# A stick-breaking attention block: the causal mask put into the scores' accumulator ahead of the scores, and the order of work planned with measured matmul times

## The chip, the cores and the metric

The kernel runs on one core of a Trainium2 chip. A time is the device time of one execution in microseconds (us). Besides it there is a trace of one profiled execution, and it is this trace that the text reads. The engines are named as the profile names them: PE does the matmuls (PEld is its weight loads), DVE is the vector engine, ACT the scalar engine, POOL is GpSimd, and SP issues most of the loads.

## The reference

One decoder layer on 256 rows of 4096 numbers, all fp32 (only the attention layer is there, since the depth is 1):

```python
def attn_branch(xn, w_in, w_out):
    proj = xn @ w_in                                  # 256x4096 @ 4096x16384
    q, k, v, g = jnp.split(proj, 4, axis=-1)
    o = stick_breaking_attention(heads(q), heads(k), heads(v))   # 32 heads of 128
    return (o * jax.nn.silu(g)) @ w_out               # 256x4096 @ 4096x4096

# stick_breaking_attention, for one block of 128 query rows:
    causal = s_pos[None, :] < t_pos[:, None]
    z = einsum('bhqd,bhkd->bhqk', qb, k) * scale
    log_fail = where(causal, log_sigmoid(-z), 0.0)
    suffix = cumsum(log_fail, reverse=True) - log_fail
    log_a = log_sigmoid(z) + suffix
    a = where(causal, exp(log_a), 0.0)
    o = einsum('bhqk,bhkd->bhqd', a, v)

h = x + attn_branch(rms_norm(x, norm_attn), w_in, w_out)
out = rms_norm(h, final_norm)
```

## The kernel before

**The two large products.** The 16384 columns of w_in are done in 16 units of 1024 columns, the 4096 columns of w_out in 4 units after them. The stationary operands are 128x128 blocks of the normalised rows (or, for w_out, of the gated head outputs), the moving operands are 128x512 blocks of weights. All units but the first of each matrix use Strassen-like forms, with fewer products and some sums of weights and of rows instead. An fp32 operand is split into a high part, rounded to the type that PE multiplies, and a low part, the rest. So a product is three matmuls into one accumulator `acc`: high weights with high rows, low weights with high rows, high weights with low rows. `mm3` issues the three. In the names of the trace, `wh` and `wl` are the high and the low part of the weights, `sh` and `sl` those of the rows in the w_in units, `oh` and `ol` those of the gated heads (`p`) in the w_out units.

**Who makes the operands.** SP loads a block `raw` of weights (a ring of 9 of them), DVE makes sums of blocks (`raw<-raw,raw`), ACT casts `wh<-raw`, and DVE subtracts `wl<-raw,wh`. At the end of a unit DVE and ACT bring the accumulators (`combine`) into `qk_sb` and `gv_sb`, or into `h` in the w_out units. There the residual (`xres`) and the gain (`grow`) are also applied to `h` on DVE, one block after the other.

**The heads.** The two heads of unit u are done while PE works on unit u+1. A head is a chain over PE, ACT and DVE (`head`, and `gated_with` for its gate): four transposes into `tr`, a copy to `qkT` on ACT, the two score matmuls into the accumulator `z`, the causal mask added to two 128x128 blocks of `z` on DVE, softplus and its split into `fh` and `fl`, four matmuls of the suffix sum into the same `z`, the exponential `a`, two transposes of the gate and two matmuls into `o`. So PE's queue gets five insertions of two or four small matmuls for each head, 160 in all. The mask is `never`, a 128x128 tile that holds a very negative number where a key isn't ahead of its query and zero elsewhere.

**What sets the order.** Every engine runs its queue in the order in which the program was written, and that order comes out of a planner (`Plan`): it plays the kernel with a cost for each piece of work (`vector_ns`, `scalar_ns`, `tensor_ns`, and for the small matmuls of the heads `ten`), and on each engine it writes next the waiting work with the lowest key. A key is mostly the place in PE's planned run at which the result is due, less a lead in us: `EARLY` for loads, `CAST_AHEAD` for casts, `SUMS_AHEAD` and `FOURTH_AHEAD` for sums of blocks, `EVICT` for bringing accumulators in, `HEADS_AHEAD` and `HEADS_LATER` for the forms of the heads for w_out. `HEAD_AT` and `GATE_AT` say after which step of unit u+1 the heads and the gate of unit u may begin. `LEAD` is what the planner lets pass between an operand's end and the product that uses it. None of this is in the program that runs: there only the order is left, and the waits on data. Since all work goes through one helper, almost every line of the trace is L167, and instructions are told apart by the tiles they write and read.

Of the kernel before, what the change touches and what calls it, by code (L numbers as in the profile page):

```python
# [14 lines left out]
ALU = mybir.AluOpType  # L15
# [4 lines left out]
P = 128  # L20
S = 256
D = 4096
H = 32
NT = S // P
KC = D // P
CW = 256
HG = CW // P
NB = D // CW
# [18 lines left out]
PAIRS, LOWS = 6, 5  # L47
KEPT = 6
LAST_STEPS = (2,6,5,1,0,7,3,4)
LATE_FROM, LATE_BEHIND = 4,1  # L50
CLOSING = "adebcf"
HEAD_AT = (1,5)
GATE_AT = 1
HEAD_SOON, GATE_SOON = 8.0,8.0

SPREAD = (10, 1.1)
HEADS_AHEAD = 4
HEADS_LATER = 10
AHEAD, SUMS_AHEAD = 1.0,3.0
PIPE = 1  # L60
T3_LEAD = 2000
FOURTH_IN, FOURTH_OUT = (5, 6),()
FOURTH_AHEAD = 10.0
RAW_LEAD = 0
EARLY = 1.5
TEN_WAIT = 1500
LAST_WAIT = 1000
QK_LEAD = 1500
CAST_AHEAD = 3.0
BLOCKS_LATER = 1  # L70
NEVER = -1e30
OUT_ACT = (1, 4, 7)
# [2 lines left out]
FORM_LEAD = 0  # L75
STATS = 2, 6
AWAY, PLACE_H = (0, 1, 2), (0, 1, 0, 1, 0, 2)
EVICT = 1500


PLAIN = {"C11": 1, "C21": 4, "C12": 7, "C22": 6}
# [60 lines left out]


def tensor_ns(n):
    return 0.4167 * n + 13.4 if n > 128 else 109.0


class Plan:
# [7 lines left out]

    TAIL = {"tensor": 190, "vector": 114, "scalar": 125, "gpsimd": 50, "sync": 50}

    LEAD = 195

    class Engine:
        def __init__(self, tc, engine):
# [120 lines left out]
def kernel(  # L283
# [124 lines left out]
        return nc.work("scalar", cost, emit, soon() if key is None else key, **kw)  # L408


    FULL_P, FULL_S = (P,) * 2, (W,) * 2

    def ten(emit, *n, last=False):
        return nc.work(
            "tensor", 90 + sum(tensor_ns(m) for m in n), emit, nc.here - 1e4, wait=LAST_WAIT if last else TEN_WAIT
        )

    def moved(engine, emit, sizes, key, after=None, hold=False, adds=False):
        issue = 700 if engine == "gpsimd" else 330
# [519 lines left out]
    def mm3(out_, a, b, start, stop):  # L939

        (ah, al), (bh, bl) = a, b
        kw = dict(skip_group_check=True)
        nc.tensor.matmul(out_, ah, bh, start=start, stop=False, **kw)
        nc.tensor.matmul(out_, ah, bl, start=False, stop=False, **kw)
        nc.tensor.matmul(out_, al, bh, start=False, stop=stop, **kw)


    BW = 3 * P
    def head(u, i):
        yield nc.take("att", "qkh")  # L950
        tr = att.tile([P, 2, S], F32, tag="att", name=f"tr{u}_{i}")

        def turn():
            for k in range(2):
                for t in range(NT):
                    c = k * CW + i * P
                    nc.tensor.transpose(tr[:, k, t * P : (t + 1) * P], st["qk", u][:, t, c : c + P], ident)

        yield ten(turn, P, P, P, P, last=u == NB - 1)
        if i == HG - 1:  # L960
            nc.give("one")
        qk = ap.tile([P, 2, S], F32, tag="qkh", name=f"qkT{u}_{i}")
        yield act(lambda: nc.scalar.copy(qk, tr), 2 * S)
        nc.give("att")
        yield nc.take("att")
        z = att.tile([P, BW], F32, tag="att", name=f"z{u}_{i}")

        def scores():
            kw = dict(stop=False, skip_group_check=True)
            nc.tensor.matmul(z[:, 0:P], qk[:, 1, P:S], qk[:, 0, P:S], start=True, **kw)  # L970
            nc.tensor.matmul(z[:, P:BW], qk[:, 1, 0:P], qk[:, 0, :], start=False, **kw)

        yield ten(scores, *FULL_P, *FULL_S, last=u == NB - 1)
        nc.give("qkh")
        yield nc.take("f")
        front = z[:, 0 : 2 * P].rearrange("p (a b) -> p a b", a=2)
        both = never.rearrange("p (a b) -> p a b", a=1).broadcast_to([P, 2, P])
        yield dve(lambda: nc.vector.tensor_tensor(out=front, in0=front, in1=both, op=ALU.add), 2 * P)

        f = ap.tile([P, BW], F32, tag="f", name=f"f{u}_{i}")  # L980

        def soft():
            nc.scalar.activation(f, z, AF.Softplus, scale=scale)

        yield act(soft, (BW, TABLE), soon(HEAD_SOON))
        yield nc.take("qkh", "gh", first=True)
        fh = ap.tile([P, BW], F32R, tag="qkh", name=f"fh{u}_{i}")
        fl = wp.tile([P, BW], F32R, tag="gh", name=f"fl{u}_{i}", bufs=3)
        yield act(lambda: nc.scalar.activation(fh, f, AF.Copy, scale=1.0 / scale), BW)
        yield dve(  # L990
            lambda: nc.vector.scalar_tensor_tensor(
                out=fl, in0=f, scalar=1.0 / scale, in1=fh.bitcast(F32), op0=ALU.mult, op1=ALU.subtract
            ),
            BW,
        )
        nc.give("f")

        def scan():
            kw = dict(start=False, skip_group_check=True)
            nc.tensor.matmul(z, neg_tri, fh, stop=False, **kw)  # L1000
            nc.tensor.matmul(z, neg_tri, fl, stop=False, **kw)
            nc.tensor.matmul(z[:, 2 * P : BW], neg_one, fh[:, 0:P], stop=False, **kw)
            nc.tensor.matmul(z[:, 2 * P : BW], neg_one, fl[:, 0:P], stop=True, **kw)

        yield ten(scan, BW, BW, P, P, last=u == NB - 1)
        nc.give("qkh", "gh")
        yield nc.take("f")
        a = ap.tile([P, BW], F32, tag="f", name=f"a{u}_{i}")


        def weights_of():
            nc.scalar.activation(a, z, AF.Relu, scale=-scale)
            nc.scalar.preload_act_table_set("natural_log_exp_and_others")
            nc.scalar.activation(a, a, AF.Exp, scale=-1.0)

        yield act(weights_of, (BW, TABLE, BW))
        nc.give("att")
        nc.start(gated_with(u, i))
        yield nc.until(("gated", u, i))
        o = st["both", u, i][:, 1, :]  # L1020
        v = lambda t: st["gv", u][:, t, i * P : (i + 1) * P]

        def out_of_head():
            kw = dict(skip_group_check=True)
            nc.tensor.matmul(o, v(0), a[:, P:BW], start=True, stop=False, **kw)
            nc.tensor.matmul(o[:, P:S], v(1), a[:, 0:P], start=False, stop=True, **kw)

        yield ten(out_of_head, *FULL_P, *FULL_S, last=u == NB - 1)
        nc.give("f")
        if i == HG - 1:  # L1030
            nc.give("two")
        gated = st["gated", u, i]
        yield dve(lambda: nc.vector.tensor_tensor(out=gated, in0=o, in1=gated, op=ALU.mult), S)
        nc.give("att")

    def gated_with(u, i):
        yield nc.until(("gate", u))
        yield nc.take("att")
        both = st["both", u, i] = att.tile([P, 2, S], F32, tag="att", name=f"o{u}_{i}")
        gT = both[:, 0, :]  # L1040

        def turn():
            for t in range(NT):
                nc.tensor.transpose(gT[:, t * P : (t + 1) * P], st["gv", u][:, t, CW + i * P : CW + (i + 1) * P], ident)

        yield ten(turn, P, P, last=u == NB - 1)
        if i == 0:
            yield nc.take("gh", first=True)
            st["o", u] = wp.tile([P, 4, P], F32, tag="gh", name=f"gated{u}", bufs=3)
        gated = st["gated", u, i] = st["o", u][:, 2 * i : 2 * i + 2, :].rearrange("p a b -> p (a b)")  # L1050
        yield act(lambda: nc.scalar.copy(gated, gT), S)
        nc.tell(("gated", u, i))
# [425 lines left out]
```

## Time and profile before

| what | value |
|---|---|
| time, median of 3 runs | 1715.29 us (1714.85 to 1718.54) |
| span of the profiled execution | 1713.9 us |
| PE busy | 1695.8 us, 99% of the span |
| DVE busy | 1626.6 us, 95% |
| ACT busy | 1299.1 us, 76% |
| POOL busy | 229.2 us, 13% |
| matmuls into acc | 1868 of each of three kinds for w_in, 485 of each of three for w_out |
| DMA | 438.82 MB, mean 256 GB/s |

The profiled execution is a single one: its span runs from the first to the last instruction and is 1.4 us under the median of the timed runs. Busy times overlap, since the engines work beside each other. A matmul's own busy time is longer than the distance to the next one, since PE is a pipeline, so in the timelines the starts of the matmuls are what is to be compared. In a row of a timeline stand the start, the busy time, the engine, the line, the operation with its tiles, and in brackets how long the engine had been idle before it and what ended the wait. A row with "x2" or more is a run of such instructions, with the busy time of all of them.

### The profile page before, as it was taken

To read this page: it belongs to the slowest core of one execution; us is meant where nothing else is said; L and a number is where in the kernel's file an instruction comes from. 1 tells how busy PE (TensorE), PEld (TensorE's weight loads), DVE (VectorE), ACT (ScalarE), POOL (GpSimd) and SP (SyncE) were. 2 spreads that over 40 slices of the span, in tenths; PEclk is the share of its full clock that TensorE was granted. 3 is DMA by queue.
4 is the path that set the end of the run, shared out by engine and by line. 5 is a ranking of instruction groups with operands and counts; after the bars stand their busy time and mean duration, and the time that the engine had idled before them with its cause. 6 is when DMAs were issued, how large, how long until landed. Compare 5 with 4: busy or idle time off the path is not lost.

```text
span 1713.9 us, 24493 instructions
## 1 busy us (share of the span) xinstructions
PE 1695.8 (99%) x7645; PEld 1401.2 (82%) x7645; DVE 1626.6 (95%) x1840; ACT 1299.1 (76%) x1579; POOL 229.2 (13%) x241
## 2 busy tenths in 40 slices
PE   9999999999999999999999999999999999999996
PEld 6888888888888888888888888888888888888885
DVE  7889999999999999999999999999999987899997
ACT  7977878777777787878787778787878875656564
POOL 0001111111111111111101010101111122011000
PEclk9999999999999999999999999999999999999998
DMA  9979898989898989898989897989898888798886
GB/s 303 359 206 261 238 264 242 268 238 272 230 276 234 278 224 284 220 286 220 282 221 287 218 284 221 279 230 267 239 265 247 275 267 247 224 283 261 259 247 236
DMA packets 243764, 438.82 MB, mean 256 GB/s; under 512 B 25616, under 2 KB 47888, under 8 KB 243632
## 3 DMA queue, kind: packets, MB, share of 16 engines
q1 hardware_dynamic: 196752, 354.24, 61.7%
q0 software_dynamic: 45584, 81.15, 26.7%
q10 hardware_dynamic: 1296, 1.85, 0.3%
q8 instruction: 60, 0.98, 0.2%
q14 instruction: 72, 0.59, 0.1%
HBM read 411.45 MB, written 9.96 MB: 246 GB/s over the span
## 4 chain that ended last, share of the span: by engine, by line
PE 96%; DVE 2%; DMA 1%; issue 0%; ACT 0%; SPq 0%; DVEq 0%; ACTq 0%
PE acc L167 91%; PE z L167 2%; PE o L167 2%; PE tr L167 1%; DVE wl L167 1%; DMA raw<-in_w_in_dram 1%; DVE h L167 1%; DMA raw<-in_w_out_dram 0%; SPq L167 0%; ACT sq L167 0%; DVE raw L167 0%; DVE p L167 0%; DVE xs L167 0%; ACT wh L167 0%; DVE back L167 0%
## 5 line engine op out<-in xcount | busy, mean ns | idle before, releaser
L167 ACT CAST wh<-raw 128x1024 fp32r<-128x1024 f32 (+1 forms) x989 | 976.1, 1016 | 323.7 <-PE acc L167 138.6
L167 DVE TENSOR_TENSOR wl<-raw,wh 128x1024 fp32r<-128x1024 f32 (+1 forms) x989 | 1130.6, 1181 | 27.6 <-ACT wh L167 17.4
L167 PE MATMUL acc<-wh,sh 128*128 128x512 f32 x1868 | 745.2, 399 | 0.7 <-ACT wh L167 0.7
L167 PE MATMUL acc<-wh,sl 128*128 128x512 f32 x1868 | 729.5, 391 | 0.4 <-DVE sl L167 0.4
L167 PE MATMUL acc<-wl,sh 128*128 128x512 f32 x1868 | 728.2, 390 | 1.0 <-DVE wl L167 1.0
L167 PEld LDWEIGHTS acc<-wh,sl 128*128 128x128 f32 x1868 | 350.8, 188 | 76.0 <-DVE sl L167 1.0
L167 PEld LDWEIGHTS acc<-wl,sh 128*128 128x128 f32 x1868 | 351.6, 188 | 71.7 <-DVE wl L167 2.5
L167 PEld LDWEIGHTS acc<-wh,sh 128*128 128x128 f32 x1868 | 351.4, 188 | 70.4 <-ACT wh L167 2.2
L167 DVE TENSOR_TENSOR raw<-raw,raw 128x512 f32<-128x512 f32 (+1 forms) x384 | 357.5, 936 | 2.2 <-issue 1.4
L167 POOL DMA_DIRECT2D raw<-in_w_in_dram x120 | 144.2, 1202 | 1073.0 <-DMA raw<-in_w_in_dram 654.6
L167 PE MATMUL acc<-wl,oh 128*128 128x512 f32 x485 | 189.4, 390 | 1.1 <-DVE wl L167 1.0
L167 PE MATMUL acc<-wh,oh 128*128 128x512 f32 x485 | 190.0, 392 | 0.0
L167 PE MATMUL acc<-wh,ol 128*128 128x512 f32 x485 | 189.2, 390 | 0.0
L167 PEld LDWEIGHTS acc<-wl,oh 128*128 128x128 f32 x485 | 91.1, 188 | 21.4 <-DVE wl L167 2.8
L167 PEld LDWEIGHTS acc<-wh,ol 128*128 128x128 f32 x485 | 91.1, 188 | 19.3 <-DVE ol L167 0.5
L167 PEld LDWEIGHTS acc<-wh,oh 128*128 128x128 f32 x485 | 91.1, 188 | 18.7
L167 ACT ACT_TABLE_LOAD x80 | 102.6, 1283 | 1.4
L167 DVE TENSOR_TENSOR gv_sb<-acc,gv_sb 128x512 f32<-128x512 f32 (+1 forms) x60 | 49.3, 822 | 19.5 <-ACT wh L167 18.2
L167 POOL DMA_DIRECT2D raw<-in_w_out_dram x18 | 21.7, 1204 | 162.0 <-DMA raw<-in_w_out_dram 105.4
L167 POOL DMA_DIRECT2D raw<-raw x30 | 26.5, 883 | 83.7 <-DMA raw<-in_w_in_dram 41.3
L167 ACT ACTIVATE qk_sb<-qk_sb,rin_v 128x512 f32<-128x512 f32 x30 | 21.6, 723 | 19.0 <-DVE qk_sb L167 19.0
L167 ACT CAST oh<-p 128x512 fp32r<-128x512 f32 (+3 forms) x41 | 19.5, 488 | 20.0 <-DVE p L167 11.2
(84 smaller groups left out, 666.2 us busy)
## 6 DMA issues: line engine op xcount, KB each, us to landing
raw<-in_w_in_dram SPq DMA_DIRECT2D x1022, 256.0 KB, 5.1
raw<-in_w_out_dram SPq DMA_DIRECT2D x256, 256.0 KB, 5.2
raw<-in_w_in_dram POOLq DMA_DIRECT2D x60, 512.0 KB, 7.9
raw<-in_w_in_dram POOLq DMA_DIRECT2D x60, 256.0 KB, 7.0
raw<-raw POOLq DMA_DIRECT2D x30, 512.0 KB, 7.5
p<-spill POOLq DMA_DIRECT2D x41, 128.0 KB, 4.8
raw<-in_w_out_dram POOLq DMA_DIRECT2D x9, 512.0 KB, 8.9
xr<-in_x_dram SPq DMA_DIRECT2D x16, 256.0 KB, 5.6
```

The lines of the kernel that those rows point to most:

```text
L167: return self.tc.keep_in_program_order(getattr(self.engine, name)(*args, **kw))
```

## The change

Four things change together.

- **The mask.** ACT copies `never` into the two blocks of `z` ahead of the score matmuls, and these accumulate onto it (`start=False`). DVE's addition to `z` is gone. The zone's flags, by which a matmul overwrites or adds, are now left to the transposes of `tr`: their order is another, and the first two of the four carry `start`.
- **The order in `mm3`.** The matmul of the low weights was the second of three and is the last now.
- **The planner's costs.** `tensor_ns` becomes 226.4 ns for 512 columns, the insertions of the heads get a number each (360, 470, 520, 575, 140 ns), and `LEAD` is 0 instead of 195 ns.
- **The planner's leads**, a dozen numbers at the head of the file.

```diff
--- before.py
+++ after.py
@@ -47,26 +47,26 @@
 PAIRS, LOWS = 6, 5
 KEPT = 6
 LAST_STEPS = (2,6,5,1,0,7,3,4)
-LATE_FROM, LATE_BEHIND = 4,1
+LATE_FROM, LATE_BEHIND = 4, 1
 CLOSING = "adebcf"
-HEAD_AT = (1,5)
-GATE_AT = 1
-HEAD_SOON, GATE_SOON = 8.0,8.0
+HEAD_AT = (3, 5)
+GATE_AT = 4
+HEAD_SOON, GATE_SOON = 6.0, 8.0
 
 SPREAD = (10, 1.1)
-HEADS_AHEAD = 4
-HEADS_LATER = 10
-AHEAD, SUMS_AHEAD = 1.0,3.0
+HEADS_AHEAD = 5
+HEADS_LATER = 5
+AHEAD, SUMS_AHEAD = 0.5, 4.0
 PIPE = 1
 T3_LEAD = 2000
 FOURTH_IN, FOURTH_OUT = (5, 6),()
-FOURTH_AHEAD = 10.0
+FOURTH_AHEAD = 14.0
 RAW_LEAD = 0
-EARLY = 1.5
+EARLY = 2.5
 TEN_WAIT = 1500
 LAST_WAIT = 1000
 QK_LEAD = 1500
-CAST_AHEAD = 3.0
+CAST_AHEAD = 5.0
 BLOCKS_LATER = 1
 NEVER = -1e30
 OUT_ACT = (1, 4, 7)
@@ -75,7 +75,7 @@
 FORM_LEAD = 0
 STATS = 2, 6
 AWAY, PLACE_H = (0, 1, 2), (0, 1, 0, 1, 0, 2)
-EVICT = 1500
+EVICT = 500
 
 
 PLAIN = {"C11": 1, "C21": 4, "C12": 7, "C22": 6}
@@ -142,7 +142,7 @@
 
 
 def tensor_ns(n):
-    return 0.4167 * n + 13.4 if n > 128 else 109.0
+    return 226.4 * n / 512
 
 
 class Plan:
@@ -156,7 +156,7 @@
 
     TAIL = {"tensor": 190, "vector": 114, "scalar": 125, "gpsimd": 50, "sync": 50}
 
-    LEAD = 195
+    LEAD = 0
 
     class Engine:
         def __init__(self, tc, engine):
@@ -408,12 +408,8 @@
         return nc.work("scalar", cost, emit, soon() if key is None else key, **kw)
 
 
-    FULL_P, FULL_S = (P,) * 2, (W,) * 2
-
-    def ten(emit, *n, last=False):
-        return nc.work(
-            "tensor", 90 + sum(tensor_ns(m) for m in n), emit, nc.here - 1e4, wait=LAST_WAIT if last else TEN_WAIT
-        )
+    def ten(emit, cost, last=False):
+        return nc.work("tensor", cost, emit, nc.here - 1e4, wait=LAST_WAIT if last else TEN_WAIT)
 
     def moved(engine, emit, sizes, key, after=None, hold=False, adds=False):
         issue = 700 if engine == "gpsimd" else 330
@@ -941,8 +937,8 @@
         (ah, al), (bh, bl) = a, b
         kw = dict(skip_group_check=True)
         nc.tensor.matmul(out_, ah, bh, start=start, stop=False, **kw)
-        nc.tensor.matmul(out_, ah, bl, start=False, stop=False, **kw)
-        nc.tensor.matmul(out_, al, bh, start=False, stop=stop, **kw)
+        nc.tensor.matmul(out_, al, bh, start=False, stop=False, **kw)
+        nc.tensor.matmul(out_, ah, bl, start=False, stop=stop, **kw)
 
 
     BW = 3 * P
@@ -951,12 +947,14 @@
         tr = att.tile([P, 2, S], F32, tag="att", name=f"tr{u}_{i}")
 
         def turn():
-            for k in range(2):
-                for t in range(NT):
-                    c = k * CW + i * P
-                    nc.tensor.transpose(tr[:, k, t * P : (t + 1) * P], st["qk", u][:, t, c : c + P], ident)
-
-        yield ten(turn, P, P, P, P, last=u == NB - 1)
+            for n, (k, t) in enumerate(((1, 0), (0, 0), (0, 1), (1, 1))):
+                c = k * CW + i * P
+                nc.tensor.matmul(
+                    tr[:, k, t * P : (t + 1) * P], st["qk", u][:, t, c : c + P], ident, start=n < 2, stop=True,
+                    is_transpose=True, skip_group_check=True,
+                )
+
+        yield ten(turn, 360, last=u == NB - 1)
         if i == HG - 1:
             nc.give("one")
         qk = ap.tile([P, 2, S], F32, tag="qkh", name=f"qkT{u}_{i}")
@@ -965,17 +963,18 @@
         yield nc.take("att")
         z = att.tile([P, BW], F32, tag="att", name=f"z{u}_{i}")
 
+        front = z[:, 0 : 2 * P].rearrange("p (a b) -> p a b", a=2)
+        both = never.rearrange("p (a b) -> p a b", a=1).broadcast_to([P, 2, P])
+        yield act(lambda: nc.scalar.copy(front, both), 2 * P)
+
         def scores():
-            kw = dict(stop=False, skip_group_check=True)
-            nc.tensor.matmul(z[:, 0:P], qk[:, 1, P:S], qk[:, 0, P:S], start=True, **kw)
-            nc.tensor.matmul(z[:, P:BW], qk[:, 1, 0:P], qk[:, 0, :], start=False, **kw)
-
-        yield ten(scores, *FULL_P, *FULL_S, last=u == NB - 1)
+            kw = dict(start=False, stop=False, skip_group_check=True)
+            nc.tensor.matmul(z[:, 0:P], qk[:, 1, P:S], qk[:, 0, P:S], **kw)
+            nc.tensor.matmul(z[:, P:BW], qk[:, 1, 0:P], qk[:, 0, :], **kw)
+
+        yield ten(scores, 470, last=u == NB - 1)
         nc.give("qkh")
         yield nc.take("f")
-        front = z[:, 0 : 2 * P].rearrange("p (a b) -> p a b", a=2)
-        both = never.rearrange("p (a b) -> p a b", a=1).broadcast_to([P, 2, P])
-        yield dve(lambda: nc.vector.tensor_tensor(out=front, in0=front, in1=both, op=ALU.add), 2 * P)
 
         f = ap.tile([P, BW], F32, tag="f", name=f"f{u}_{i}")
 
@@ -1002,7 +1001,7 @@
             nc.tensor.matmul(z[:, 2 * P : BW], neg_one, fh[:, 0:P], stop=False, **kw)
             nc.tensor.matmul(z[:, 2 * P : BW], neg_one, fl[:, 0:P], stop=True, **kw)
 
-        yield ten(scan, BW, BW, P, P, last=u == NB - 1)
+        yield ten(scan, 520, last=u == NB - 1)
         nc.give("qkh", "gh")
         yield nc.take("f")
         a = ap.tile([P, BW], F32, tag="f", name=f"a{u}_{i}")
@@ -1025,7 +1024,7 @@
             nc.tensor.matmul(o, v(0), a[:, P:BW], start=True, stop=False, **kw)
             nc.tensor.matmul(o[:, P:S], v(1), a[:, 0:P], start=False, stop=True, **kw)
 
-        yield ten(out_of_head, *FULL_P, *FULL_S, last=u == NB - 1)
+        yield ten(out_of_head, 575, last=u == NB - 1)
         nc.give("f")
         if i == HG - 1:
             nc.give("two")
@@ -1043,7 +1042,7 @@
             for t in range(NT):
                 nc.tensor.transpose(gT[:, t * P : (t + 1) * P], st["gv", u][:, t, CW + i * P : CW + (i + 1) * P], ident)
 
-        yield ten(turn, P, P, last=u == NB - 1)
+        yield ten(turn, 140, last=u == NB - 1)
         if i == 0:
             yield nc.take("gh", first=True)
             st["o", u] = wp.tile([P, 4, P], F32, tag="gh", name=f"gated{u}", bufs=3)
```

The queues hold the same instructions as before, but for 32 additions `z<-z,never` that leave DVE and 32 copies `z<-never` of 128x256 that come to ACT. What moves is their order.

On PE, at the ninth block of weights of the first unit (`wh8`, `wl8`; `sh4` and `sl4` are the rows' forms for it), before:

```order
L167 MATMUL acc0_6_197<-wh7_286,sl3_96 128x512
L167 MATMUL acc0_1_130<-wh8_303,sh4_298 128x512
L167 MATMUL acc0_1_130<-wl8_312,sh4_298 128x512
L167 MATMUL acc0_1_130<-wh8_303,sl4_299 128x512
L167 MATMUL acc0_4_170<-wh8_303,sh4_298 128x512
L167 MATMUL acc0_4_170<-wl8_312,sh4_298 128x512
L167 MATMUL acc0_4_170<-wh8_303,sl4_299 128x512
```

and now:

```order
L167 MATMUL acc0_6_197<-wl7_302,sh3_95 128x512
L167 MATMUL acc0_1_130<-wh8_306,sh4_298 128x512
L167 MATMUL acc0_1_130<-wh8_306,sl4_299 128x512
L167 MATMUL acc0_1_130<-wl8_312,sh4_298 128x512
L167 MATMUL acc0_4_169<-wh8_306,sh4_298 128x512
L167 MATMUL acc0_4_169<-wh8_306,sl4_299 128x512
L167 MATMUL acc0_4_169<-wl8_312,sh4_298 128x512
```

In each group of three the matmul of `wl` has gone from the second to the third place, and that of `sl` from the third to the second.

On DVE, at the start of the first unit of w_out (unit 16), while the heads of unit 15 are still to be done, before:

```order
L167 TENSOR_TENSOR gv_sb15_12569<-acc15_3_11942,gv_sb15_12569 128x512
L167 TENSOR_TENSOR wl814_12665<-raw128_10_12553,wh814_12647 128x1024
L167 TENSOR_TENSOR p0_12519<-p0_12519 128x128 x4
L167 TENSOR_TENSOR p1_12527<-p1_12527 128x2x128
L167 TENSOR_TENSOR p2_12626<-p2_12626 128x128 x4
L167 TENSOR_TENSOR z15_0_12732<-z15_0_12732,never_122 128x256
L167 TENSOR_TENSOR ol0_12602<-p0_12519,oh0_12601 128x384
L167 TENSOR_TENSOR ol1_12611<-p1_12527,oh1_12610 128x256
L167 TENSOR_TENSOR ol2_12708<-p2_12626,oh2_12707 128x384
L167 TENSOR_TENSOR wl815_12685<-raw128_11_12562,wh815_12664 128x1024
L167 TENSOR_TENSOR wl816_12697<-raw129_00_12570,wh816_12684 128x1024
```

and now:

```order
L167 TENSOR_TENSOR wl813_12653<-raw128_01_12498,wh813_12631 128x1024
L167 TENSOR_TENSOR gv_sb15_12590<-acc15_5_11937,gv_sb15_12590 128x1024
L167 TENSOR_TENSOR p1_12515<-p1_12515 128x2x128
L167 TENSOR_TENSOR gv_sb15_12590<-acc15_3_11941,gv_sb15_12590 128x512
L167 TENSOR_TENSOR ol0_12601<-p0_12507,oh0_12600 128x384
L167 TENSOR_TENSOR ol1_12612<-p1_12515,oh1_12611 128x256
L167 TENSOR_TENSOR wl814_12670<-raw128_10_12540,wh814_12645 128x1024
L167 TENSOR_TENSOR wl815_12688<-raw128_11_12554,wh815_12669 128x1024
L167 TENSOR_TENSOR ol2_12752<-p2_12684,oh2_12751 128x512
L167 TENSOR_TENSOR wl816_12701<-raw129_00_12570,wh816_12687 128x1024
L167 TENSOR_TENSOR p2_12684<-p2_12684 128x128 x4
L167 TENSOR_TENSOR wl817_12725<-raw129_01_12583,wh817_12698 128x1024
```

`p0` to `p2` are the first blocks of gated heads for w_out. Before, `wl815` stands behind ten additions on `p`, the mask of the first head of unit 15 and three `ol`; now the two additions on `gv_sb15` and two `ol` stand ahead of `wl814`, `wl815` follows it at once, the mask is gone and the additions on `p2` come later.

On DVE, in the second unit of w_out, before:

```order
L167 TENSOR_TENSOR wl863_13833<-raw139_01_13754,wh863_13814 128x1024
L167 TENSOR_TENSOR wl864_13848<-raw138_11_13673,wh864_13831 128x512
L167 TENSOR_TENSOR h0_1_13566<-h0_1_13566,xres0_1_13818 128x512
L167 TENSOR_TENSOR wl865_13867<-raw139_11_13763,wh865_13847 128x1024
L167 TENSOR_TENSOR raw139_00_13712<-raw139_00_13712,raw139_10_13630 128x1024
L167 TENSOR_TENSOR h0_1_13566<-h0_1_13566,grow0_13726 128x512
L167 TENSOR_TENSOR wl866_13878<-raw139_10_13630,wh866_13866 128x1024
L167 TENSOR_TENSOR raw139_11_13763<-raw139_00_13712,raw139_11_13763 128x1024
L167 TENSOR_TENSOR wl867_13910<-raw139_00_13712,wh867_13877 128x1024
```

and now:

```order
L167 TENSOR_TENSOR raw139_00_13712<-raw139_00_13712,raw139_10_13606 128x1024
L167 TENSOR_TENSOR h0_1_13567<-h0_1_13567,xres0_1_13818 128x512
L167 TENSOR_TENSOR wl864_13848<-raw138_11_13673,wh864_13831 128x512
L167 TENSOR_TENSOR wl865_13863<-raw139_11_13766,wh865_13847 128x1024
L167 TENSOR_TENSOR h0_1_13567<-h0_1_13567,grow0_13726 128x512
L167 TENSOR_TENSOR wl866_13875<-raw139_10_13606,wh866_13862 128x1024
L167 TENSOR_TENSOR wl867_13891<-raw139_00_13712,wh867_13874 128x1024
L167 TENSOR_TENSOR raw139_11_13766<-raw139_00_13712,raw139_11_13766 128x1024
L167 TENSOR_TENSOR wl868_13902<-raw140_00_13777,wh868_13888 128x1024
```

The sum `raw139_00` has gone ahead of the addition of `xres0_1`, and the sum `raw139_11` behind `wl867`.

## The prediction

> **What bounds the kernel now.** I read the page first, for the engines and the chain of waits; these are its span, its busy times and the chain:
>
> ```profile
> span 1713.9 us, 24493 instructions
> PE 1695.8 (99%) x7645; PEld 1401.2 (82%) x7645; DVE 1626.6 (95%) x1840; ACT 1299.1 (76%) x1579; POOL 229.2 (13%) x241
> PE 96%; DVE 2%; DMA 1%; issue 0%; ACT 0%; SPq 0%; DVEq 0%; ACTq 0%
> ```
>
> PE holds 96% of the chain that ended last. Then the busy time by stretches (us, then busy time and instructions of PE, PEld, DVE, ACT and POOL, granted clock, DMA share, GB/s):
>
> ```profile
> 0.00:85.00 85.00, 81.61 (x338) 63.00 (x339) 69.07 (x133) 71.46 (x139) 3.68 (x12) 1.00 0.97 331
> 1020.00:1190.00 170.00, 170.00 (x776) 141.24 (x775) 166.11 (x175) 133.57 (x152) 24.20 (x23) 1.00 0.90 249
> 1360.00:1530.00 170.00, 168.93 (x752) 138.48 (x751) 147.26 (x206) 114.15 (x153) 30.24 (x47) 1.00 0.80 247
> 1530.00:1700.00 170.00, 169.97 (x750) 140.36 (x748) 162.59 (x184) 102.03 (x125) 14.40 (x13) 1.00 0.83 250
> ```
>
> In the middle PE has no idle time at all: 170.00 of 170, with the heads' small matmuls in it. So the time is made of PE's own instructions, which the change leaves as they are, and of three other things: the waits of the start (3.4 us of idle in the first 85), some in the w_out units, and 13.9 us behind 1700. DVE, at 166 of 170, has hardly 4 us to spare there, and ACT 36.
>
> **The start.** PE's and DVE's rows show several waits of this kind up to 33 us; the last one is, on PE:
>
> ```profile
> 32.06 0.40 PE L167 MATMUL acc<-wl,sh 128*128 128x512 f32 x1
> 32.83 0.50 PE L167 MATMUL acc<-wh,sl 128*128 128x512 f32 x1 [0.37 <-DVE sl L167]
> 33.17 0.39 PE L167 MATMUL acc<-wh,sh 128*128 128x512 f32 x1
> 33.40 0.40 PE L167 MATMUL acc<-wl,sh 128*128 128x512 f32 x1
> ```
>
> DVE works without a gap from 20 us to here and its order in the first 40 or so instructions doesn't change, so `sl` comes at 32.83 whatever PE did before. Now `wh,sl` is the second of its three and `wl,sh` still stands behind it: one matmul more after 32.83, **+0.23 us** (33.17 to 33.40, the distance of two matmuls that wait for nothing). Earlier waits on `wl` get 0.23 shorter, but all of them are absorbed by this one.
>
> **The mask.** It comes off DVE and goes to ACT; the nearest row for the copy is the copy of the same shape out of the accumulators:
>
> ```profile
> L167 DVE TENSOR_TENSOR z<-z,never 128x256 f32<-128x256 f32 x32 | 13.8, 432 | 0.0
> L167 ACT COPY gated<-o 128x256 f32<-128x256 f32 x32 | 11.6, 364 | 0.0
> ```
>
> DVE gets back at most 32 x 0.432 = 13.8 us. ACT takes on 32 copies of 0.364 to, at most, the 0.432 that DVE needs for the same shape, so 11.6 to 13.8 us; I take 0.364, the plain copy. Two heads fall in each unit of some 85 us: 0.73 us of the 18 us in which ACT idles there. PE waits for neither engine in the middle, so the sum has **0** for both; without ACT's idle time the copies would cost up to 11.6. The score matmuls now wait for the copy, which stands behind `qkT`'s on the same engine. PE's five insertions for each head keep their matmuls. They come six to eight products after one another now, from the transposes to the scores, four or five before, and none but one `o` (below) waited before: **0**; with that cover gone, each `z` would wait 0.36 us, 11.6 in all.
>
> **The third matmul of a product.** `wl` is needed 0.23 us later, `sl` and `ol` 0.23 us earlier. In the middle it is `wl` that comes closest, at the change of units, where DVE also brings in the accumulators:
>
> ```profile
> 682.58 1.42 DVE L167 TENSOR_TENSOR gv_sb<-acc,gv_sb 128x512 f32<-128x512 f32 x2 [1.35 <-ACT wh L167]
> 692.05 1.22 DVE L167 TENSOR_TENSOR wl<-raw,wh 128x1024 fp32r<-128x1024 f32 x1
> ```
>
> ```profile
> 684.12 0.39 PE L167 MATMUL acc<-wh,sl 128*128 128x512 f32 x1
> 692.06 0.39 PE L167 MATMUL acc<-wl,sh 128*128 128x512 f32 x1
> 694.10 0.39 PE L167 MATMUL acc<-wl,sh 128*128 128x512 f32 x1
> ```
>
> The `wl` of 692.05 ends at 693.27, 0.83 us ahead of its matmul at 694.10: the least lead of the unit, and so it is in the others. 0.23 more where nothing waits is worth **0**. But the smaller `EVICT` puts five pieces of work (two bringings-in of 0.60 and 1.13, one more of 0.60, two sums of 0.60) between two `wl` that stood side by side. The second of them is then the critical one, the `wl` whose matmul starts at 692.06. The stretch ahead of it begins where the accumulator of `qk_sb`'s addition is full, behind PE's matmul of 684.12, at about 684.5. From there DVE has four bringings-in and two sums of 0.60 each, one bringing-in of 1.13, one `wl` of 1.13, and the last `wl` of 1.22: 7.1 us, so it ends at 691.6. Its matmul, at 692.06 + 0.23, comes 0.65 us later, 0.5 to 0.8 with the inaccuracy of such a reading. Still no wait, so **0**, but here is the first rival.
>
> **The waits of the w_out units.** Five, and one at an insertion. The largest two, first on PE and then on DVE:
>
> ```profile
> 1371.34 0.39 PE L167 MATMUL acc<-wh,oh 128*128 128x512 f32 x1
> 1372.12 0.51 PE L167 MATMUL acc<-wl,oh 128*128 128x512 f32 x1 [0.40 <-DVE wl L167]
> 1372.46 0.40 PE L167 MATMUL acc<-wh,ol 128*128 128x512 f32 x1
> ...
> 1491.13 0.39 PE L167 MATMUL acc<-wh,oh 128*128 128x512 f32 x1
> 1492.13 0.50 PE L167 MATMUL acc<-wl,oh 128*128 128x512 f32 x1 [0.61 <-DVE wl L167]
> 1492.46 0.39 PE L167 MATMUL acc<-wh,ol 128*128 128x512 f32 x1
> ```
>
> ```profile
> 1367.73 1.60 DVE L167 TENSOR_TENSOR p<-p 128x256 f32<-128x256 f32 x5
> 1369.25 0.42 DVE L167 TENSOR_TENSOR z<-z,never 128x256 f32<-128x256 f32 x1
> 1369.58 1.35 DVE L167 TENSOR_TENSOR ol<-p,oh 128x384 fp32r<-128x384 f32 x3
> 1370.85 2.35 DVE L167 TENSOR_TENSOR wl<-raw,wh 128x1024 fp32r<-128x1024 f32 x2
> ...
> 1485.10 0.69 DVE L167 TENSOR_TENSOR h<-h,xres 128x512 f32<-128x512 f32 x1 [0.99 <-DMA xres<-in_x_dram]
> 1490.86 2.35 DVE L167 TENSOR_TENSOR wl<-raw,wh 128x1024 fp32r<-128x1024 f32 x2
> ```
>
> At 1371 the matmuls start 0.78 and then 0.34 apart instead of 0.23: 0.55 + 0.11 = 0.67 us lost. The 0.11 is the weight load, which waits with its matmul:
>
> ```profile
> 1492.12 0.19 PEld L167 LDWEIGHTS acc<-wl,oh 128*128 128x128 f32 x1 [1.03 <-DVE wl L167]
> ```
>
> By the Trainium skill (TensorE: Matmul & The Clock Gate, "Step-by-step: what each phase is for") PE pulls a weight load ahead of matmuls in flight where it goes to the background weight buffer; by it the load of `oh` would be done during the wait, and each wait cost 0.11 less. This row speaks against it here, since its load, which doesn't read `wl`, waited for `wl` too; by the page the five waits would be worth 1.9 instead of 2.4 us.
>
> At 1371, `wl815` now follows `wl814` at once; the mask (0.33 from start to start) is out of the way, and the last `ol2` (0.45, a third of the 1.35) and the sums of `p2` (four of the five in 1.60) come behind. These are some 2 us, more than the 0.55, so this wait goes: **-0.67** (at worst 0, if the two additions on `gv_sb15`, now ahead, come late). At 1491 the loss is 0.77 + 0.11 = 0.88. DVE had lost 0.99 to a late `xres`; a sum of 1.13 us now stands ahead of that wait and fills it, and another goes behind `wl867`; I take **-0.7**, with 0 and -0.88 as the ends. The other four, on PE:
>
> ```profile
> 1393.09 0.39 PE L167 MATMUL acc<-wh,ol 128*128 128x512 f32 x1
> 1393.44 0.92 PE L167 MATMUL o<-a,gv_sb 128*128 128x256 f32 x4
> ...
> 1435.26 0.39 PE L167 MATMUL acc<-wl,oh 128*128 128x512 f32 x1
> 1435.68 0.50 PE L167 MATMUL acc<-wh,ol 128*128 128x512 f32 x1
> ...
> 1524.00 0.39 PE L167 MATMUL acc<-wh,oh 128*128 128x512 f32 x1
> 1524.42 0.50 PE L167 MATMUL acc<-wl,oh 128*128 128x512 f32 x1
> ...
> 1573.31 0.39 PE L167 MATMUL acc<-wh,oh 128*128 128x512 f32 x1
> 1573.72 0.50 PE L167 MATMUL acc<-wl,oh 128*128 128x512 f32 x1
> ```
>
> `o` starts late by 0.12 and its load shows the rest, in all 0.2 over its 31 likes; its head's chain is shorter by the mask: **-0.2** (0 to -0.23). The one at 1435 (0.42 - 0.23 + 0.11 = 0.30) waits for `ol`, which is now due 0.23 sooner: **+0.25** (0 to +0.5). The last two wait for `wl` by 0.19, less than the 0.23 that the new place gives, so they go with their reload: **-0.5** (0 to -0.6).
>
> **The end.** From the last product to the last store DVE's and ACT's orders are the old ones: **0** of the 13.9 us, which begin at about 1700.
>
> **The sum.** +0.23 - 0.67 - 0.7 - 0.2 + 0.25 - 0.5 = -1.6 us: a span of 1712.3. The profiled span before is 1.4 us under the median of its runs; with the same distance the time is **1713.7 us**. From the bounds of the terms: -2.1 at best, +0.7 at worst, so 1713.2 to 1716.0 for this case.
>
> **The rivals.** *Slower: PE waits for `wl` at every change of units.* The new lead of 0.65 us is used up as soon as the bringing-in begins that much later, and it hangs on ACT too, which makes the first half of it: one cast of 1.05 us more ahead of ACT's part puts `wl` 0.40 behind its matmul. With the reload that is 0.5 us in each of 15 units, +7.6, or 1721.3; it decides from 0.65 us on. For it speaks that DVE has no slack inside that stretch, whatever it saves elsewhere; against it, that ACT idles a fifth of the time and that before, too, a lead of 0.83 held in every unit. Chance 0.14. *Faster: the start shrinks as well.* The waits up to 33 us come to 3.4 us of idle in the first row of the stretches, and reloads. If ACT and DVE are held there by PE's giving buffers back, and not by the loads, the earlier waits on `wl`, shorter by 0.23 each, let everything move up, and 2 to 3 us go beside the late ones: 1710.7 to 1711.7. DVE's gapless run from 20 to 33 us speaks against it, and DMA at 0.97 of the time in that stretch. Chance 0.12. *The late waits only move.* Each of the `wl` waits becomes one for `ol`, or for the next operand of the same busy DVE (147 of 170 us there, but in bursts): only the start's term is left, 1715.5. Chance 0.18.
>
> **How the numbers follow.** The forecast has 0.56. A difference under about 0.2%, 3.4 us, can't be told from none; forecast and moved waits both lie inside, so same is 0.74, faster 0.12, slower 0.14. The range takes in the faster case and of the slower one what stays under 0.3 us in each unit (15 x 0.3 = 4.5 over the forecast): 1710.0 to 1718.0; the forecast's own is 1713.2 to 1716.0.
>
> **What would show it.** Right: PE busy 170.00 of 170 in the middle again; no wait at 1371, 1491, 1524 and 1573; `wh,sl` as the last wait of the start, near 32.8; a copy `z<-never` of about 0.36 us on ACT; 13.9 us from the last product on. Wrong: waits of PE for `wl` that come back every 85 us, a first stretch with PE busy above 82.5 us, or an insertion `z` that waits for ACT.

## The result: 0.3% slower

The changed kernel takes 1722.46 us (median of 15 runs, 1715.64 to 1726.55), the kernel before beside it 1716.65 us (15 runs, 1714.85 to 1719.08). The ratio is 1.0031, with a 95% interval of 1.0023 to 1.0039. Forecast were 1713.7 us and no difference; the range ended at 1718.0. Two things are to be explained: some 5 us more, and runs that lie 11 us apart instead of 4.

The profiled execution has a span of 1718.6 us, 4.7 more than before. It is a single one, and took 2.1 us less than the median. The page of the changed kernel, its span, its busy times and the chain of waits:

```profile
span 1718.6 us, 24606 instructions
PE 1698.1 (99%) x7645; PEld 1398.7 (81%) x7645; DVE 1619.8 (94%) x1808; ACT 1294.0 (75%) x1611; POOL 229.6 (13%) x241
PE 94%; DMA 2%; DVE 2%; ACT 1%; issue 1%; SPq 0%; POOL 0%; DVEq 0%; ACTq 0%; POOLq 0%
```

DVE is 7 us less busy, half of the 13.8 us that the 32 masks had in their own row, and PE's share of the chain is 94% instead of 96%: DMA, which had 1%, has 2 now. By stretches (the columns are those of the prediction's table):

```profile
0.00:85.00 85.00, 79.93 (x338) 62.49 (x339) 69.20 (x134) 72.07 (x139) 4.11 (x12) 1.00 0.97 329
680.00:850.00 170.00, 169.36 (x768) 139.34 (x767) 163.53 (x168) 131.80 (x157) 23.63 (x22) 1.00 0.89 251
850.00:1020.00 170.00, 169.62 (x767) 139.00 (x766) 163.20 (x169) 131.85 (x156) 23.53 (x22) 1.00 0.89 249
1360.00:1530.00 170.00, 169.26 (x758) 139.77 (x757) 148.15 (x209) 115.32 (x157) 31.41 (x50) 1.00 0.82 255
1530.00:1700.00 170.00, 170.00 (x751) 140.53 (x751) 163.68 (x174) 103.45 (x120) 14.36 (x13) 1.00 0.84 256
```

The two stretches of the middle in the kernel before:

```profile
680.00:850.00 170.00, 170.00 (x776) 141.22 (x776) 165.88 (x174) 134.64 (x154) 23.93 (x22) 1.00 0.92 254
850.00:1020.00 170.00, 170.00 (x776) 141.25 (x775) 165.17 (x173) 133.75 (x154) 24.86 (x23) 1.00 0.91 254
```

The w_out units (1360 on) are a little better than before, as forecast. The middle isn't: PE now idles there, and in 170 us it runs 767 or 768 instructions instead of 776.

To compare kernels I add up, over PE's rows, what each distance between two matmuls has more than 0.227 us (the distance of two that wait for nothing), and what each insertion of a head has more than most of its kind. This is the time that PE lost, reloads of weights included. It explains all spans here: span less lost time is 1705.1 to 1706.4 us in every kernel of this study. So PE's own work and the end are the same everywhere to 1.3 us, and what differs is in these columns (us; the start is up to 85 us, the w_out units from 1360 on):

| kernel | start | middle | w_out | sum | span | ratio to before, 95% interval |
|---|---|---|---|---|---|---|
| before | 5.2 | 0.0 | 2.7 | 7.9 | 1713.9 | |
| changed | 4.9 | 6.5 | 1.4 | 12.8 | 1718.6 | 1.0031 (1.0023 to 1.0039) |
| changed, EARLY 1.5 | 5.7 | 0.0 | 7.9 | 13.7 | 1719.5 | 1.003 (1.002 to 1.004) |
| before, EARLY 2.5 | 5.2 | 1.3 | 8.6 | 15.1 | 1720.8 | 1.0038 (1.0025 to 1.0051) |
| mask and order of the three only | 5.9 | 0.7 | 3.6 | 10.1 | 1715.3 | 1.0001 (0.9993 to 1.001) |
| planner's costs and leads only | 5.4 | 14.6 | 15.8 | 35.9 | 1742.0 | 1.0143 (1.013 to 1.0156) |
| changed, EARLY 1.5, heads' numbers of before | 5.2 | 3.1 | 4.5 | 12.8 | 1719.1 | 1.0042 (1.003 to 1.0053) |
| changed, light accumulating loads | 5.3 | 0.0 | 0.9 | 6.2 | 1711.3 | 0.9975 (0.9965 to 0.9985) |
| changed, heads' numbers of before | 5.4 | 3.3 | 4.8 | 13.5 | 1719.9 | 1.002 (1.0011 to 1.0029) |
| before, light accumulating loads | 5.4 | 0.0 | 2.1 | 7.5 | 1713.1 | 0.9985 (0.9975 to 0.9995) |
| mask, order and costs, leads of before | 7.4 | 7.8 | 5.3 | 20.6 | 1726.6 | 1.0074 (1.0056 to 1.0092) |
| changed, EARLY 0.5 | 5.1 | 19.6 | 6.3 | 31.1 | 1737.4 | 1.0134 (1.0118 to 1.015) |
| changed, EARLY 1.5 up to unit 13 | 5.2 | 2.3 | 5.0 | 12.4 | 1718.3 | 1.0009 (1.0 to 1.0018) |
| changed, EARLY 1.5 in the w_in units | 5.5 | 0.9 | 5.4 | 11.8 | 1717.7 | 1.0021 (1.0011 to 1.0031) |

**Where it is lost in the middle.** Not at the change of units, where the forecast's first rival had it, but 22 to 26 us behind the first matmul of a unit, in seven of the fourteen units from 170 us on, and three times at an insertion `z` some 32 us behind it. One such place, first on PE, then on ACT and DVE:

```profile
794.01 0.39 PE L167 MATMUL acc<-wh,sl 128*128 128x512 f32 x1
794.74 0.50 PE L167 MATMUL acc<-wl,sh 128*128 128x512 f32 x1 [0.34 <-DVE wl L167]
...
796.63 0.50 PE L167 MATMUL acc<-wl,sh 128*128 128x512 f32 x1 [0.22 <-DVE wl L167]
```

```profile
791.42 4.84 ACT L167 CAST wh<-raw 128x1024 fp32r<-128x1024 f32 x5 [5.05 <-DMA raw<-in_w_in_dram]
```

```profile
790.65 1.22 DVE L167 TENSOR_TENSOR raw<-raw,raw 128x1024 f32<-128x1024 f32 x1
793.45 1.23 DVE L167 TENSOR_TENSOR wl<-raw,wh 128x1024 fp32r<-128x1024 f32 x1 [1.59 <-ACT wh L167]
```

Read backwards: PE waits for `wl`, DVE had stood 1.59 us for `wh`, and ACT had stood 5.05 us for a load. The block was issued at 783.9 and landed at 791.3; the same block in the kernel before was issued at 783.4 and landed at 786.8, and its cast is the last of a row of five without a wait:

```profile
783.81 5.00 ACT L167 CAST wh<-raw 128x1024 fp32r<-128x1024 f32 x5
```

Beside it in the changed kernel flew one of GpSimd's accumulating loads (782.9 to 789.6), which in the kernel before came at 784.8 and hit the next block. ACT's waits for loads, as a row of the table of waits (us in total, times, longest), before and now:

```profile
ACT wh L167 <- DMA raw<-in_w_in_dram: 24.0, 20, 2.6
```

```profile
ACT wh L167 <- DMA raw<-in_w_in_dram: 74.8, 55, 5.1
```

### The profile page after: what moved, and what is told of

It reads as the page before. It is cut to its first block, busy times and chain, and to the rows that moved or that the text cites. A ratio compares the mean times of both kernels' runs of the same rounds, so it can differ in the third digit from the quotient of the medians.

```text
span 1718.6 us, 24606 instructions
## 1 busy us (share of the span) xinstructions
PE 1698.1 (99%) x7645; PEld 1398.7 (81%) x7645; DVE 1619.8 (94%) x1808; ACT 1294.0 (75%) x1611; POOL 229.6 (13%) x241
## 2 busy tenths in 40 slices
DMA packets 243764, 438.82 MB, mean 255 GB/s; under 512 B 25616, under 2 KB 47888, under 8 KB 243632
## 4 chain that ended last, share of the span: by engine, by line
PE 94%; DMA 2%; DVE 2%; ACT 1%; issue 1%; SPq 0%; POOL 0%; DVEq 0%; ACTq 0%; POOLq 0%
PE acc L167 89%; PE z L167 2%; PE o L167 2%; DMA raw<-in_w_in_dram 1%; PE tr L167 1%; DVE wl L167 1%; ACT wh L167 1%; DMA p<-spill 1%; DVE raw L167 0%; DVE h L167 0%; DMA raw<-in_w_out_dram 0%; SPq L167 0%; DVE back L167 0%; POOL p L167 0%; ACT oh L167 0%
## 5 line engine op out<-in xcount | busy, mean ns | idle before, releaser
L167 ACT CAST wh<-raw 128x1024 fp32r<-128x1024 f32 (+1 forms) x989 | 965.2, 1015 | 313.1 <-DVE raw L167 126.1
```

What stands on the lines that cost most here:

```text
L167: return self.tc.keep_in_program_order(getattr(self.engine, name)(*args, **kw))
```

## The experiments

**Theories.** The weights come in sets of four blocks, (0,0) to (1,1), eight sets in a unit of w_in. Theory L: loads land late, because `EARLY` moves the block (1,0) of each set of four, and with it the accumulating load that it releases, to a place where it slows a load that is due at once. Theory E: the order of DVE at the change of units, or that of the casts, makes `wl` late by itself. Theory M: the mask or the order of the three matmuls does it.

### EARLY alone, in both kernels

```diff
-EARLY = 2.5
+EARLY = 1.5
```

> The changed kernel with one number put back: EARLY = 1.5. Theory L (loads): with 2.5 the block (1,0) of each set of four is loaded a place sooner, takes a buffer of the ring for longer, and the blocks behind it come late; with 1.5 the waits of PE in the middle (3.8 us in twelve places between 289 and 1309) go and the time falls by 4 to 7 us, to about 1715 to 1717, ratio to before 0.998 to 1.001. Theory E (the order of DVE at the change of units, EVICT and the casts) and theory M (mask and order of the three matmuls): no change, ratio 1.002 to 1.004.

Measured: 1721.9 us, ratio 1.003. The waits in the middle went, 0.0 us of 6.5 are left. But the time did not follow: in the w_out units 7.9 us are lost instead of 1.4.

```diff
-EARLY = 1.5
+EARLY = 2.5
```

> The kernel before with one number changed: EARLY = 2.5. Theory L: it gets the waits in the middle that the changed kernel has, +3 to +6 us, ratio 1.002 to 1.004. Theories E and M: same as before, ratio 0.999 to 1.001.

This is the kernel before. Measured: 1723.43 us, ratio 1.0038: as theory L has it in the time, but only 1.3 us of it are in the middle, 8.6 in the w_out units. So with 2.5 the kernel before loses 7 us more, while the changed kernel with 1.5 gives its 6.5 back elsewhere: where it is paid depends on the rest of the order.

What it does to the blocks (0,1) is alike in all kernels. Some 106 of them are issued between 170 and 1300 us in each; their issues, landings and casts in the trace are told apart by the order of the program. With 1.5 throughout the w_in units, 5 to 13 of them fly longer than 6.5 us, and at the median they lie ready 2.7 to 3.5 us ahead of their cast. With 2.5 and full loads, 34 to 47 fly that long, and 1.3 to 2.5 us of reserve are left. In the order of the loads (0,1) stands behind (1,0) with 2.5, and ahead of it with 1.5.

### The parts apart

Mask and `mm3` of the changed kernel, all costs and leads of before:

```diff
-EARLY = 2.5
+EARLY = 1.5
...
-    LEAD = 0
+    LEAD = 195
```

> The mask on ACT and the new order of the three matmuls, with the planner's costs and leads of before. Theory L and theory E: within 1.5 us of before (ratio 0.999 to 1.001), PE without a wait in the middle. Theory M: slower by 4 to 6 us, since the scores wait for ACT or sl comes late.

Measured: ratio 1.0001 (0.9993 to 1.001). Theory M falls; the forecast's 0 for these two parts holds.

The reverse, costs and leads alone, with the mask on DVE and `wl` in the second place:

```diff
-        nc.tensor.matmul(out_, al, bh, start=False, stop=False, **kw)
-        nc.tensor.matmul(out_, ah, bl, start=False, stop=stop, **kw)
+        nc.tensor.matmul(out_, ah, bl, start=False, stop=False, **kw)
+        nc.tensor.matmul(out_, al, bh, start=False, stop=stop, **kw)
```

> The new costs and leads of the planner alone, mask on DVE and the old order of the three matmuls. Theory L and theory E: slower than before by 5 us or more (ratio 1.003 or above), since wl is needed 0.23 us sooner and DVE has the mask as well. Theory M: the same as before.

Measured: ratio 1.0143, 24 us. Here there is a wait at the change of every unit, for an accumulator that DVE brings in too late. DVE and PE, unit 7:

```profile
695.95 0.68 DVE L167 TENSOR_TENSOR qk_sb<-acc,gv_sb 128x512 f32<-128x512 f32 x1
```

```profile
696.14 0.39 PE L167 MATMUL acc<-wh,sl 128*128 128x512 f32 x1
696.69 0.50 PE L167 MATMUL acc<-wh,sh 128*128 128x512 f32 x1 [0.16 <-DVE qk_sb L167]
```

It repeats in each unit within a few hundredths of a microsecond, 1 us with a second one and the reloads, 14.6 us in all. The 15.8 us of the w_out units are another thing: most of them, some 9 us, are lost from 1376 to 1388, in and behind one insertion of the last heads. So the leads need the time that the mask gives back to DVE, or the later `wl`; which of the two, these runs don't say.

The measured matmul times without the new leads:

```diff
-EARLY = 2.5
+EARLY = 1.5
...
-EVICT = 500
+EVICT = 1500
```

> Mask on ACT, the new order of the three matmuls and the measured matmul times, with all the leads of before. If the measured times alone make the plan worse on the chip: ratio 1.002 or more. If the leads do (EARLY above all): within 2 us of before, ratio 0.998 to 1.001, at most 1 us of waits in the middle.

Measured: ratio 1.0074, 12 us slower, with a wait for `wl` in thirteen units a few us behind their change and some 2 us more in the start. A plan that is truer to PE was worse on the chip with leads that had been set under the other costs. The expectation that the leads alone do it falls.

### The loads, with every queue in its order

This is the run that tells L from E, since nothing is reordered: the accumulating loads fill 32 partitions instead of 128, so that three quarters of these sums of weights are left out.

```diff
-                r[:, :, 0:n, :], w[b : c + 1 : c - b, s, :, HALF : HALF + n, :]...
+                r[0:32, :, 0:n, :], w[b : c + 1 : c - b, s, 0:32, HALF : HALF + n, :]...
```

> The changed kernel, every queue in the same order; only the accumulating loads of GpSimd move 32 of 128 partitions, so that part of the sums of weights is left out. Theory L (a load that lands late because it is in flight beside an accumulating one): PE's waits in the middle go from 6.5 us to under 1, loads land in 3 to 5 us instead of up to 7 or 8, and the span falls by 5 to 7 us, to 1712 to 1714. Theory that the order on DVE or ACT itself is late: the waits in the middle stay at 5 us or more.

Measured: 1712.93 us (1712.59 to 1713.73), ratio 0.9975. The same two stretches as above:

```profile
680.00:850.00 170.00, 170.00 (x776) 141.22 (x775) 165.12 (x170) 133.10 (x157) 18.54 (x22) 1.00 0.76 225
850.00:1020.00 170.00, 170.00 (x776) 141.20 (x775) 164.90 (x170) 134.06 (x158) 18.44 (x22) 1.00 0.75 227
```

PE is at 170.00 of 170 again, all 6.5 us of the middle are gone, and the runs lie 1.1 us apart instead of 11. Of the blocks (0,1), 7 instead of 47 fly longer than 6.5 us. So the loads' time in flight makes the waits in the middle and the spread of the runs: shown, not argued.

But the (0,1) are not the blocks that PE waits for. The load at 791 us is the block (1,1) of the third set of its unit, and by the order of the program every wait of PE for `wl` in the middle of the changed kernel stands behind this block. In the fourteen units from 170 us on, by issue and landing in the traces:

| kernel | GpSimd's load is issued | the block flies, us | ACT has stood idle ahead of its cast, us |
|---|---|---|---|
| before | 1.1 to 1.9 us behind it, once 3.7 | 3.1 to 5.6 | 0 to 1.2 |
| changed | 0.2 to 1.7 us ahead of it | 4.5 to 7.5 | 2.1 to 5.1 |
| changed, EARLY 1.5 | 1.0 to 2.2 us behind it | 3.2 to 5.4 | 0.8 to 3.1 |
| changed, light accumulating loads | 1.4 to 1.9 us ahead of it | 3.4 to 5.2 | 1.0 to 2.8 |

In the seven units in which PE waited for `wl`, ACT had stood 3.9 to 5.1 us, in the other seven 2.1 to 3.9. The first three kernels move the same 438.82 MB, the light one 398.12: so what counts is a full accumulating load issued just ahead of this block, and not the sum of traffic. It also fits that 2.5 in the kernel before costs only 1.3 us in the middle: GpSimd's load is issued there from 0.5 us ahead of this block to 0.9 behind it.

> The kernel before, queues in the same order, with accumulating loads of 32 of 128 partitions, as in the light form of the changed kernel. Theory L: before had hardly a wait for loads in the middle, so it gains much less than the changed kernel did: 0 to 3 us, ratio 0.998 to 1.000, and the light form of the changed kernel (0.9975) is then the faster of the two by 1 to 3 us, which is what the mask and the orders are worth. If every kernel gains the same 6 to 9 us from lighter loads, the loads don't explain the difference: ratio 0.995 or less.

The same lighter loads in the kernel before. Measured: 1714.98 us (1713.17 to 1716.09), ratio 0.9985. By the medians it gains 2.7 us on the kernel before in its own comparison (1717.69), less than the 9.5 by which the light form of the changed kernel is under 1722.46, as expected. Light against light the changed kernel is 2.05 us the shorter by the medians, and 1.8 by the spans; the forecast had -1.6. The ratios' intervals overlap, so this difference is likely rather than certain.

ACT's row of waits in the light form of the changed kernel is a warning against reading totals:

```profile
ACT wh L167 <- DMA raw<-in_w_in_dram: 63.4, 52, 2.9
```

It still waits 52 times and 63 us for loads, against 20 times and 24 us in the kernel before (`CAST_AHEAD`, the lead of the casts, is 5 instead of 3 us), and PE loses nothing by it. What counts is the longest wait, 2.9 instead of 5.1.

### The heads' numbers, and other places for the block

```diff
-HEAD_AT = (3, 5)
-GATE_AT = 4
-HEAD_SOON, GATE_SOON = 6.0, 8.0
+HEAD_AT = (1, 5)
+GATE_AT = 1
+HEAD_SOON, GATE_SOON = 8.0, 8.0
...
-HEADS_AHEAD = 5
-HEADS_LATER = 5
+HEADS_AHEAD = 4
+HEADS_LATER = 10
```

> The changed kernel with the heads' numbers of before, EARLY left at 2.5. Theory L: the middle keeps 3 to 8 us of waits, ratio 1.002 to 1.004. If the heads' places in the units make the middle slow: no waits there, ratio 0.999 to 1.001.

Measured: ratio 1.002; 3.3 us lost in the middle, irregular as in the changed kernel, and 4.8 in the w_out units. The heads don't make the middle slow; the new numbers are worth about 3 us in the w_out units, but only with `EARLY` at 2.5 (1.4 against 4.8): with 1.5 they cost as much there (7.9 against 4.5, the next run).

> The changed kernel with EARLY = 1.5 and the heads' numbers of before (HEAD_AT, GATE_AT, HEAD_SOON, HEADS_AHEAD, HEADS_LATER). Two causes (loads in the middle, late forms of the heads at the start of the w_out units): with both put back PE's waits come to 8 us or less in all (start 5.5, middle under 0.5, w_out 2 to 3) and the time is that of before or up to 2 us less, ratio 0.998 to 1.000. If another number (casts, sums, EVICT, costs) is the cause: ratio 1.002 to 1.004 as with EARLY alone.

With both put back: ratio 1.0042. I had expected 8 us of lost time, it is 12.8, and the profiled execution is the fastest of the six, 4.2 us under their median. The middle is nearly free of late loads, but it has the forecast's first rival, in its place and in nearly every unit:

```profile
693.85 0.39 PE L167 MATMUL acc<-wh,sl 128*128 128x512 f32 x1
694.19 0.50 PE L167 MATMUL acc<-wl,sh 128*128 128x512 f32 x1
```

0.12 and a reload of 0.11, thirteen times: 3.1 us.

```diff
-EARLY = 2.5
+EARLY = 0.5
```

> The changed kernel with EARLY = 0.5: the block (1,0), and with it the accumulating load, starts two places later than in the changed kernel, behind the last block of the four before. Theory L with the collision as its cause: the late block is then (0,0), which has 1 us or more to spare, the middle keeps less than 1 us of waits and the time is 1714 to 1718, ratio 0.998 to 1.001. If any place of the accumulating load is as bad, since it is the traffic as such: ratio 1.002 to 1.004.

Measured: ratio 1.0134. My idea that a later accumulating load meets a block with more reserve was wrong as a way to a faster kernel: few (0,1) loads fly long (9 of 105), yet 19.6 us are lost in the middle, mostly in waits of 0.6 to 1.6 us for `wl` near the change of units. There the planner had shifted the work of DVE, and the first rival is there with a higher price.

Two last runs tried to take each stage from the kernel that does it best:

```diff
-                tiles.append((4 * q + k - (EARLY if seven[q] and not k else 0), q, *tile_))
+                tiles.append((4 * q + k - ((1.5 if q < 14 * NS else EARLY) if seven[q] and not k else 0), q, *tile_))
```

> The changed kernel with EARLY = 1.5 in the first 14 units of w_in and 2.5 behind them, to take the middle of the kernel with 1.5 (0.03 us of waits) and the w_out units of the changed kernel (1.4 us). If the two stages can be had apart: PE waits 5.5 + under 1 + 1.5 to 3 us, 7 to 9 in all, and the time is that of before, ratio 0.998 to 1.001. If the w_out units only come out well with the delays that the changed kernel has in the middle: 4 us or more of waits there, ratio 1.001 to 1.004.

> The same with 1.5 in all 16 units of w_in and 2.5 in the w_out units alone. The waits of the kernel with 1.5 throughout begin at 1386, where loads for the plain unit 16, which has no such block, are under way: so most of its 5.6 us in the w_out units stay, ratio 1.001 to 1.003. If the blocks of the units behind 16 cause them: 1.5 to 3 us of waits there and ratio 0.998 to 1.001.

The second has 16 in place of 14. Measured: ratios 1.0009 and 1.0021. The middle is nearly clean up to the switch (0.0 and 0.9 us; in the first kernel 2.3 us from 1216 on, where 2.5 already holds, behind the block (1,1) of the third set again), but the w_out units lose 5 us, and don't come out as in the changed kernel. No version here that makes all the sums beats the kernel before.

**What stays open:** why the w_out units lose 4.5 to 8 us in every kernel with `EARLY` at 1.5 and the other new leads, while the changed kernel loses 1.4. In the rows PE waits there for `oh` and `ol`, ACT for `p<-spill`; that these transfers are late because of the weights' loads beside them is likely, since the light form loses 0.9 us there, but wasn't taken apart. Of the other leads (`CAST_AHEAD`, `SUMS_AHEAD`, `FOURTH_AHEAD`, `EVICT`) none was put back alone.

## Why the prediction was wrong

**PE's own work and the end: right.** Span less lost time is 1706.0 before and 1705.8 after.

**The start, +0.23: wrong in sign, small.** `sl` came at 32.52 instead of 32.83, so "`sl` comes at 32.83 whatever PE did before" didn't hold to 0.3 us; 0.2 us less is lost.

**The mask: right in price, nearly right in effect.** The copies, as a group, and who waited for them, from the rows of that tile:

```profile
L167 ACT COPY z<-never 128x256 f32<-128x256 f32 x32 | 12.0, 374 | 0.5
```

```profile
  PEld z L167: 1.1, 3
```

0.374 us is between the bounds of 0.364 and 0.432. Three insertions waited, one of the prediction's signs of being wrong, 0.7 us in all beyond their kind; in the light form none did, so it was the late loads in ACT's queue that the copy stood behind.

**The third matmul and the change of units: right, to the hundredth.** The critical `wl` is the first of these two, and its matmul:

```profile
691.01 2.35 DVE L167 TENSOR_TENSOR wl<-raw,wh 128x1024 fp32r<-128x1024 f32 x2
```

```profile
692.88 0.39 PE L167 MATMUL acc<-wl,sh 128*128 128x512 f32 x1
```

It ends at 692.23, 0.65 us ahead; 0.65 was worked out, and it is 0.65 in ten of the fourteen units (0.12 and 0.28 in two, more in the first two). So the first rival didn't occur here, though three relatives of this kernel have waits in that place.

**The w_out units: right in sum without the loads.** The waits at 1371, 1491, 1524 and 1573 are gone, and that of `o` too. The term for `ol` (+0.25 at 1435) was too small:

```profile
1440.54 0.39 PE L167 MATMUL acc<-wl,oh 128*128 128x512 f32 x1
1441.44 0.50 PE L167 MATMUL acc<-wh,oh 128*128 128x512 f32 x1 [0.51 <-ACT oh L167]
1442.17 0.50 PE L167 MATMUL acc<-wh,ol 128*128 128x512 f32 x1 [0.22 <-DVE ol L167]
```

0.67 for `oh`, 0.50 for `ol` and the reload, 1.29 instead of 0.55; ACT had waited 1.04 us for a `p` from DRAM. 2.7 became 1.4 where 0.9 was forecast, and the light form has the 0.9, 0.6 of it at this `ol`.

**The step that failed** is the one in "What bounds the kernel now" that lists what the time is made of: PE's instructions and "three other things". The loads are not among them. The sum gave the middle 0 in two terms, the mask's and the third matmul's, each reckoned on DVE and ACT with their operands there in time; and the edits of `EARLY` and `FOURTH_AHEAD`, which move transfers, got no term at all. What the runs showed in its place: with `EARLY` at 2.5 GpSimd's accumulating load is issued just ahead of a block that ACT needs at once, and this block flies 4.5 to 7.5 us instead of 3.1 to 5.6, and PE waits for the `wl` made behind it. Measured, the middle is +6.5 us in the profiled execution, and with -0.2 at the start and -1.3 in the w_out units that is the +5. The quoted rows had the hint: a DMA share of 0.90 in the very stretch in which PE had no idle time. The reserve between landing and cast, which the trace of before could have shown for each block, would have been the row to ask for: for the (1,1) of the third set it is 0.1 to 1.4 us there, against medians of 1.8 for all (1,1) and 3.3 for (0,1).

**The rivals.** "Slower" had the sign and, by luck, almost the time (1721.3, measured 1722.46), but the wrong cause and place. "Faster" and "the late waits only move" did not come: the start kept 4.9 of its 5.2 us, and the late waits went.

## What to carry to other kernels

Where the busiest engine has no idle time and DMA is at 90%, a change of the order has a term for the loads: for each block take the time from landing to first use, place by place and not by kinds, and see what else is in flight when it is issued. A reserve that is smaller than the scatter of the flight times is a cost that comes and goes from run to run; a wider spread of the runs was its mark here, and a run with the same order and lighter transfers shows it in one stroke. Leads of a planner are set together with its costs: the costs without the leads, costs and leads without the mask and the order, and one lead moved too far the other way were much worse here (ratios 1.0074, 1.0143 and 1.0134) than the whole (1.0031).

## What the runs showed of the hardware

**A wait of PE can cost as much again in clock.** In the kernel with `EARLY` at 1.5 up to unit 13, PE stood still for about 2.2 us at 1437 and 0.5 at 1439; then its granted clock (the third number from the end of a row, ahead of the DMA share) was 0.50 for some 3 us, with matmuls 0.43 us apart:

```profile
1436.50:1440.50 4.00, 1.76 (x7) 0.93 (x6) 3.24 (x6) 2.15 (x4) 2.29 (x4) 0.99 0.85 298
1440.50:1443.50 3.00, 3.00 (x9) 2.32 (x8) 2.90 (x7) 1.36 (x2) 1.17 (x3) 0.50 0.86 136
```

In the kernel with `EARLY` at 1.5 and the old heads' numbers, a wait of 2.1 us at 1440 left it as it was:

```profile
1440.00:1443.00 3.00, 1.05 (x5) 0.62 (x4) 2.93 (x7) 0.97 (x2) 2.36 (x5) 1.00 0.61 186
1443.00:1447.00 4.00, 4.00 (x20) 3.28 (x19) 3.52 (x7) 2.04 (x4) 1.55 (x2) 1.00 1.00 275
```

It happened at the start of another kernel too (mask, order and costs: 1.6 us of wait at 21.3, then eight matmuls 0.43 apart, 1.6 us more). In the kernel with the costs and leads alone the clock fell to 0.50 at 1378.8, behind an idle time of 1.23 us at 1376 and in one of 0.58 us, and stayed there for 17.1 us with idle times of 1.4, 3.6 and 2.2 us in between. The Trainium skill (TensorE: Matmul & The Clock Gate, "What's actually happening") has the clock follow the activity in a free-running window of about 3.4 us. That such waits sometimes cost the clock and sometimes not fits this, and so does the length of the slow spells by the clock's record, twice 3.41 us and once 17.07, five times as much; here a wait of 1.6 us, with a small one before it, was enough.
